# Moving operands at multiples of 1 KiB in SBUF, weight tiles 64 bytes past one, small tiles in a pool of their own

## The chip, the cores and the metric

The kernel runs on one core of one Trainium2 chip. The metric is the device time of one execution in microseconds (us). Before the change it is 2237.5 us, the median of three runs that lie between 2237.05 and 2237.68 us.

## The reference

The reference is a decoder trunk of two layers for one sequence of 256 tokens and width 2048. Layer 0 mixes with a short convolution and a gated linear attention, layer 1 with a dilated sliding-window attention of 16 heads; each is followed by an MLP of width 8192 with a squared ReLU, and a last RMSNorm ends it. What costs time is the weight matrices: about 400 MB of float32 weights, each used once, against 256 token columns.

```python
def reference(x, norm_mix_g, norm_mlp_g, final_norm_g, hyb_w_in, ..., mlp_w1, mlp_w2):
    for layer in range(DEPTH):
        h = rmsnorm(x, norm_mix_g[layer])
        if layer % 2 == 0:
            mix = conv_gla_mixer(h, hyb_w_in[e], ..., hyb_w_out[e])
        else:
            mix = dilated_attention(h, attn_w_qkv[o], attn_w_o[o])
        x = x + mix
        x = x + squared_relu_mlp(rmsnorm(x, norm_mlp_g[layer]), mlp_w1[layer], mlp_w2[layer])
    return rmsnorm(x, final_norm_g)
```

## The kernel before

Activations stand transposed in SBUF: 128 features of a k-block on the partitions, the 256 tokens along them. A float32 product is built from three products in the type float32r. Each value is split into a high part, rounded to float32r, and a low part, the rest; the kernel adds high by high, high by low and low by high in PSUM. So each activation block is a tile of 512 columns, 256 high and 256 low (2 KiB in a partition): `xs0` to `xs15` for the input of a mixer or of an MLP's first product, `ys0` to `ys15` for a mixer's output, and `hs0` to `hs15`, in the same places as `ys`, for a chunk of the MLP's hidden layer.

The weights come in steps of 128 x 1024 float32 (512 KiB, 4 KiB in a partition). For each of 770 steps SP issues the load into a ring of four `raw` tiles (line 114), ScalarE copies it rounded into a `wh` tile (line 119), VectorE subtracts that from the raw values into a `wl` tile (line 125); `wh` and `wl` are rings of five, filled four steps ahead of TensorE. Their order is that of the Python loop over `steps` at the end of `trunk_kernel`; a manual schedule keeps every engine in the order in which the program was written.

TensorE's work is nearly all in three forms, which all issue through the helper at line 128:

- `sub_a` (tile `acc` in the profile): a 128 x 128 piece of `wh` or `wl` is the stationary operand and the 256 high or low columns of an activation tile are the moving one. A step has eight such pieces and each takes three matmuls, in the order (`wh`, high), (`wh`, low), (`wl`, high): 24 matmuls a step.
- `sub_b` (tile `accv`), for the value projections: the roles are exchanged. 128 token columns of `xs` are stationary, 512 columns of `wh` or `wl` (2 KiB) move.
- `sub_g` (tile `accg`), as `sub_a`, for the gate projection and the last quarter of the last product.

```python
    def three(p, wh, wl, rhs, start, stop):
        hi, lo = rhs[:, :T], rhs[:, T:]
        mm(p, wh, hi, start, False)
        mm(p, wh, lo, False, False)
        mm(p, wl, hi, False, stop)
```

An MLP goes in four chunks: four groups of eight steps make 2048 hidden features from `xs` (768 matmuls), then four groups of eight steps take these, as `hs`, into the output (768 matmuls). The output projections of the two mixers read `ys` (768 matmuls each). All other products read `xs`.

Where a tile lies in a partition is set by the pools, one after the other in the order in which they are opened, and inside a pool by the order in which tiles are first asked for; each tile's length is rounded up to 32 bytes. The pool `const` holds `vec`, `cm` and `ones` (424, 1024 and 4 bytes), then `x`, `xs`, `ssq`, the two buffers of `rc` (8 bytes each, line 246), `rb`, `rb2` and `ys`; the pool `wts` with the rings follows, then `tmp`.

Of the kernel before, what the change touches and what calls it, by code (L numbers as in the profile page):

```python
# [11 lines left out]
F32 = mybir.dt.float32  # L12
# [6 lines left out]
P = 128  # L19
# [17 lines left out]
N_VEC = 106  # L37
# [12 lines left out]
def trunk_kernel(ctx: ExitStack, tc, xin, vecs, w_in, w_gate, w_gate2, w_out, w_qkv, w_o, w1, w2, w2f,  # L50
# [2 lines left out]
    pe, dve, act, pool = nc.tensor, nc.vector, nc.scalar, nc.gpsimd  # L53
    PSUM = bass.MemoryType.PSUM

    const = ctx.enter_context(tc.tile_pool(name="const", bufs=1))
    wts = ctx.enter_context(tc.tile_pool(name="wts", bufs=1))
    tmp = ctx.enter_context(tc.tile_pool(name="tmp", bufs=2))
# [5 lines left out]
    def bank(name):  # L64
        return psum.tile([P, 512], F32, tag="ps", name=name)


    vec = const.tile([P, N_VEC], F32, name="vec")
    cm = const.tile([P, 2, P], F32, name="cm")
    ident, cums = cm[:, 0, :], cm[:, 1, :]  # L70
    ones = const.tile([P, 1], F32, name="ones")
    x = const.tile([P, NK, T], F32, name="x")

    gpool = tc.alloc_tile_pool(name="gla", bufs=1)
# [52 lines left out]
    def mm(out_, lhsT, rhs, start, stop):  # L127
        pe.matmul(out_, lhsT=lhsT, rhs=rhs, start=start, stop=stop, skip_group_check=True)  # L128
# [95 lines left out]
    R = {}  # L224

    def rsqrt_cols(dst, src, scale, n):

        v = tmp.tile([P, 8], F32, tag="rv", name="rv")[:, :n]
        a = tmp.tile([P, 8], F32, tag="ra", name="ra")[:, :n]
        dve.tensor_scalar(v, src, scale, EPS, op0=OP.mult, op1=OP.add)  # L230
        act.activation(a, v, AF.Sqrt)
        dve.reciprocal(dst, a)
        dve.tensor_tensor(a, dst, dst, op=OP.mult)
        dve.tensor_tensor(a, a, v, op=OP.mult)
        dve.tensor_scalar(a, a, -0.5, 1.5, op0=OP.mult, op1=OP.add)
        dve.tensor_tensor(dst, dst, a, op=OP.mult)

    def norm_factor(last=False):

        p = bank("pss")  # L240
        for tt in range(2):
            for a in ssq["all"]:
                mm(p[:, tt:tt + 1], a[:, tt * P:(tt + 1) * P], ones, a is ssq["all"][0],
                   a is ssq["all"][-1])
        yield 1
        c = R["c"] = const.tile([P, 2], F32, tag="rc", bufs=2, name="rc")
        rsqrt_cols(c, p[:, :2], 1.0 / D, 2)
        yield 7
        p = bank("prb")
        for tt in range(2):  # L250
            pe.matmul(p[:, tt * P:(tt + 1) * P], lhsT=c[:, tt:tt + 1].to_broadcast([P, P]),
                      rhs=ident, start=True, stop=True)
        R["ps"] = p
        if last:
            return
        yield 1
        b = R["b"] = const.tile([P, T], F32, tag="rb", bufs=2, name="rb")
        act.activation(b, p[:, :T], AF.Copy)
        b2 = R["b2"] = const.tile([P, T], F32, tag="rb2", bufs=2, name="rb2")
        dve.tensor_tensor(b2, b, b, op=OP.mult)  # L260
        yield 1
# [17 lines left out]
    def residual(k, p, col=None, last=False, mlp=False):  # L279
        if mlp:  # L280
            t = tmp.tile([P, T], F32, tag="t", bufs=3, name="t")
            dve.tensor_tensor(t, p, R["b2"], op=OP.mult)  # L282
            p = t
        dve.tensor_tensor(x[:, k, :], x[:, k, :], p, op=OP.add)  # L284
        if col is not None:
            def rest():
                if last:
                    if k == 0:
                        fp = ctx.enter_context(
                            tc.tile_pool(name="fin", bufs=1, reuse_waits="tile"))  # L290
                        xf["x"] = fp.tile([P, NK, T], F32, name="xf")
                    if k == NK - 1:
                        sq = tmp.tile([P, T], F32, tag="sq", name="sq")
                        act.activation(sq, x[:, k, :], AF.Square)
                        ssq["all"].append(sq)
                    else:
                        square_sum(k)
                    act.activation(xf["x"][:, k, :], x[:, k, :], AF.Copy,
                                   scale=vec[:, col + k:col + k + 1])
                else:  # L300
                    scale_split(k, col)
                    square_sum(k)
                if k == NK - 1 and not last:
                    spawn(norm_factor(), 15)
            later.append(rest)
# [395 lines left out]
    def first_norm():  # L701
        for k in range(12, NK):
            square_sum(k, 12)
            yield 2
        ssq["all"] = [ssq["a"], ssq["p"]]
        yield 8
        yield from norm_factor()
# [43 lines left out]
    for _ in norm_factor(last=True):  # L751
        pass
# [97 lines left out]
```

## Time and profile before

| what | value |
|---|---|
| median of three runs | 2237.5 us |
| the profiled execution's own time | 2238.15 us |
| its span in the profile | 2236.2 us |
| TensorE matmuls busy | 2220.1 us, 99% of the span, 18390 records |
| TensorE weight loads busy | 2188.7 us, 98% |
| VectorE busy | 1326.2 us, 59% |
| ScalarE busy | 1039.4 us, 46% |
| DMA | 411.86 MB, mean 184 GB/s |

The span reaches from the first to the last instruction of the program; the time of an execution has some 2 us around it. A matmul's busy time is modelled to its end and overlaps with that of the next ones, so the pace of TensorE is read from the starts of the matmuls and from their counts, and not from the mean length of one. Where the listing of the timeline merges neighbours, a row's start is that of the first of them.

### The profile page before, as it was taken

The numbers are of one execution on the slowest core, as the hardware profiler recorded it, in microseconds if no ns is written. First come the engines' busy times: TensorE is split into PE (matmuls) and PEld (weight loads), VectorE is DVE, ScalarE is ACT, GpSimd is POOL, SyncE is SP. The second block draws the span as 40 slices with busy tenths as digits, with TensorE's granted clock in tenths as the row PEclk, the third lists the DMA queues.
The fourth block names the chain that finished last, engine by engine and source line by source line (L and its number), as shares of the span: only waits on it lengthen the run. The fifth ranks groups of instructions, "written<-read, shape, count | busy, mean of one in ns | idle before, by whom it ended". The sixth has DMA issues, their size and how long they took to land.

```text
span 2236.2 us, 43375 instructions
## 1 busy us (share of the span) xinstructions
PE 2220.1 (99%) x18390; PEld 2188.7 (98%) x18390; DVE 1326.2 (59%) x1809; ACT 1039.4 (46%) x1414; POOL 67.2 (3%) x70
## 2 busy tenths in 40 slices
PE   9999999999999999999999999999999999999997
PEld 8999999999999999999999999999999999999997
DVE  7666666555555555556665655565555555555555
ACT  6555545453444354345444444455434434534453
POOL 4001120000000000000000000000000000000000
PEclk9999999999999999999999999999999999999999
DMA  7555565566565656665655555556566666566653
GB/s 259 160 170 168 169 192 178 191 190 194 173 207 186 186 182 199 181 196 175 195 187 171 174 181 164 179 179 197 182 189 187 198 180 190 188 190 187 196 182 114
DMA packets 114405, 411.86 MB, mean 184 GB/s; under 512 B 12817, under 2 KB 13201, under 8 KB 114210
## 3 DMA queue, kind: packets, MB, share of 16 engines
q1 hardware_dynamic: 113760, 408.47, 58.1%
q8 instruction: 144, 2.36, 0.4%
q10 hardware_dynamic: 450, 0.61, 0.1%
q14 instruction: 51, 0.42, 0.1%
HBM read 406.94 MB, written 2.10 MB: 183 GB/s over the span
## 4 chain that ended last, share of the span: by engine, by line
PE 98%; DVE 1%; DMA 1%; issue 0%; SPq 0%; ACT 0%; DVEq 0%; ACTq 0%
PE acc L128 88%; PE accv L128 6%; PE accg L128 1%; PE psc L445 1%; PE pao L128 0%; DVE wl L125 0%; DVE xs L199 0%; DMA raw<-w_in 0%; PE pqk L580 0%; PE po L128 0%; PE ppt L598 0%; DVE xf L756 0%; DMA x<-xin 0%; PE pqk L579 0%; PE pos L128 0%
## 5 line engine op out<-in xcount | busy, mean ns | idle before, releaser
L125 DVE TENSOR_TENSOR wl<-raw,wh 128x1024 fp32r<-128x1024 f32 (+1 forms) x771 | 939.6, 1229 | 756.0 <-ACT wh L119 754.8
L119 ACT ACTIVATE wh<-raw 128x1024 fp32r<-128x1024 f32 (+1 forms) x771 | 810.6, 1056 | 903.9 <-PE acc L128 801.5
L128 PE MATMUL acc<-xs,wh 128*128 128x256 f32 x6400 | 1101.2, 277 | 0.1
L128 PEld LDWEIGHTS acc<-xs,wh 128*128 128x128 f32 x6400 | 965.8, 188 | 1.8 <-ACT wh L119 0.8
L128 PE MATMUL acc<-xs,wl 128*128 128x256 f32 x3200 | 885.2, 277 | 2.8 <-DVE wl L125 2.8
L128 PE MATMUL acc<-hs,wh 128*128 128x256 f32 x3968 | 714.4, 283 | 0.0
L128 PEld LDWEIGHTS acc<-hs,wh 128*128 128x128 f32 x3968 | 618.8, 192 | 0.0
L128 PEld LDWEIGHTS acc<-xs,wl 128*128 128x128 f32 x3200 | 601.0, 188 | 4.4 <-DVE wl L125 4.4
L128 PE MATMUL acc<-hs,wl 128*128 128x256 f32 x1984 | 561.5, 283 | 0.0
L128 PEld LDWEIGHTS acc<-hs,wl 128*128 128x128 f32 x1984 | 380.8, 192 | 0.0
L128 PE MATMUL acc<-ys,wh 128*128 128x256 f32 x1024 | 185.3, 284 | 0.0
L128 PEld LDWEIGHTS acc<-ys,wh 128*128 128x128 f32 x1024 | 159.8, 192 | 0.1
L128 PE MATMUL acc<-ys,wl 128*128 128x256 f32 x512 | 144.9, 283 | 0.0
L128 PE MATMUL accv<-wh,xs 128*128 128x512 f32 x384 | 122.0, 399 | 0.0
L271 DVE TENSOR_TENSOR hs<-u,hs 128x256 fp32r<-128x256 f32 x128 | 54.4, 425 | 79.0 <-ACT hs L270 79.0
L128 PEld LDWEIGHTS acc<-ys,wl 128*128 128x128 f32 x512 | 98.2, 192 | 0.0
L270 ACT ACTIVATE hs<-u 128x256 fp32r<-128x256 f32 x128 | 53.3, 417 | 71.0 <-DVE u L622 71.0
L128 PEld LDWEIGHTS accv<-wh,xs 128*128 128x128 f32 x384 | 70.3, 188 | 14.5 <-issue 0.8
L128 PE MATMUL accv<-wl,xs 128*128 128x512 f32 x192 | 75.5, 393 | 0.0
L284 DVE TENSOR_TENSOR x<-x,t 128x256 f32<-128x256 f32 x128 | 54.4, 425 | 4.4
L622 DVE TENSOR_TENSOR u<-u 128x256 f32<-128x256 f32 x128 | 53.5, 418 | 0.0
L282 DVE TENSOR_TENSOR t<-acc,rb 128x256 f32<-128x256 f32 x124 | 51.7, 417 | 0.0
(148 smaller groups left out, 793.8 us busy)
## 6 DMA issues: line engine op xcount, KB each, us to landing
raw<-w SPq DMA_DIRECT2D x504, 512.0 KB, 4.2
raw<-w_qkv SPq DMA_DIRECT2D x96, 512.0 KB, 3.6
raw<-w_in SPq DMA_DIRECT2D x95, 512.0 KB, 3.8
raw<-w_out SPq DMA_DIRECT2D x32, 512.0 KB, 3.8
raw<-w_o SPq DMA_DIRECT2D x32, 512.0 KB, 3.6
raw<-w2f SPq DMA_DIRECT2D x8, 512.0 KB, 3.8
x<-xin SPq DMA_DIRECT2D x8, 256.0 KB, 5.9
out_dram<-xf SPq DMA_DIRECT2D x7, 256.0 KB, 2.3
```

What stands on the lines that cost most here:

```text
L119: act.activation(his[s][:, c], raws[s][:, c], AF.Copy)
L125: dve.tensor_tensor(los[s][:, c], r[:, c], his[s][:, c].bitcast(F32), op=OP.subtract)
L128: pe.matmul(out_, lhsT=lhsT, rhs=rhs, start=start, stop=stop, skip_group_check=True)
L270: act.activation(t[:, :T], v, AF.Copy)
L271: dve.tensor_tensor(t[:, T:], v, t[:, :T].bitcast(F32), op=OP.subtract)
L282: dve.tensor_tensor(t, p, R["b2"], op=OP.mult)
L284: dve.tensor_tensor(x[:, k, :], x[:, k, :], p, op=OP.add)
L445: pe.matmul(p[:, (2 * h + tt) * P:(2 * h + tt + 1) * P], lhsT=l[:, h, c], rhs=r[:, h, c], start=True, stop=True)
L622: dve.tensor_tensor(u, u, u, op=OP.mult)
```

## The change

No instruction is added, removed or moved on any engine, and no wait is changed; only addresses in SBUF differ. A pool `small` is opened first and takes `vec`, `cm`, `ones` and the `rc` buffers. A tile of 88 float32 that nothing reads fills it up to a multiple of 1 KiB, and another of 16 float32 (64 bytes) stands at the head of the pool of the weight rings.

```diff
@@ -53,6 +53,9 @@
+    small = ctx.enter_context(tc.tile_pool(name="small", bufs=1))
     const = ctx.enter_context(tc.tile_pool(name="const", bufs=1))
     wts = ctx.enter_context(tc.tile_pool(name="wts", bufs=1))
     tmp = ctx.enter_context(tc.tile_pool(name="tmp", bufs=2))
@@ -65,10 +68,12 @@
-    vec = const.tile([P, N_VEC], F32, name="vec")
-    cm = const.tile([P, 2, P], F32, name="cm")
+    vec = small.tile([P, N_VEC], F32, name="vec")
+    cm = small.tile([P, 2, P], F32, name="cm")
     ident, cums = cm[:, 0, :], cm[:, 1, :]
-    ones = const.tile([P, 1], F32, name="ones")
+    ones = small.tile([P, 1], F32, name="ones")
+    small.tile([P, 88], F32, name="fill")
+    wts.tile([P, 16], F32, name="fill2")
     x = const.tile([P, NK, T], F32, name="x")
@@ -243,7 +248,7 @@
-        c = R["c"] = const.tile([P, 2], F32, tag="rc", bufs=2, name="rc")
+        c = R["c"] = small.tile([P, 2], F32, tag="rc", bufs=2, name="rc")
```

Where tiles begin, in bytes past a multiple of 1 KiB. All tiles named in a row have lengths that are multiples of 1 KiB, so each buffer of a row begins at the same remainder; a piece of a weight tile begins there or 512 bytes further, and so do the two 128-column pieces of a high or low part that `sub_b` loads.

| tiles | before | after |
|---|---|---|
| `x`, `xs` and `ssq` | 608 | 0 |
| `rb`, `rb2`, `ys` and `hs` | 672 | 0 |
| `raw`, `wh` and `wl` | 672 | 64 |
| `sq` and `u` in `tmp` | 736 | 128 |
| `v` of the value projections | 864 | 256 |
| `osq` and most other GLA tiles | 864 or 896 | 256 or 288 |

Before, `rc` takes two times 32 bytes between `ssq` and `rb`, which is why `ys` begins 64 bytes later in its KiB than `xs`.

## Rows read from the trace of the kernel before

**Rows 1.** The page's busy times: engine, us, share of the span, instructions.
```profile
PE 2220.1 (99%) x18390; PEld 2188.7 (98%) x18390; DVE 1326.2 (59%) x1809; ACT 1039.4 (46%) x1414; POOL 67.2 (3%) x70
```
**Rows 2.** The page's chain that ended last: shares by engine, then by line.
```profile
PE 98%; DVE 1%; DMA 1%; issue 0%; SPq 0%; ACT 0%; DVEq 0%; ACTq 0%
PE acc L128 88%; PE accv L128 6%; PE accg L128 1%; PE psc L445 1%; PE pao L128 0%; DVE wl L125 0%; DVE xs L199 0%; DMA raw<-w_in 0%; PE pqk L580 0%; PE po L128 0%; PE ppt L598 0%; DVE xf L756 0%; DMA x<-xin 0%; PE pqk L579 0%; PE pos L128 0%
```
**Rows 3.** Groups of TensorE's matmuls: busy us, mean ns, idle before.
```profile
L128 PE MATMUL acc<-xs,wh 128*128 128x256 f32 x6400 | 1101.2, 277 | 0.1
L128 PE MATMUL acc<-xs,wl 128*128 128x256 f32 x3200 | 885.2, 277 | 2.8 <-DVE wl L125 2.8
L128 PE MATMUL acc<-hs,wh 128*128 128x256 f32 x3968 | 714.4, 283 | 0.0
L128 PE MATMUL acc<-hs,wl 128*128 128x256 f32 x1984 | 561.5, 283 | 0.0
L128 PE MATMUL acc<-ys,wh 128*128 128x256 f32 x1024 | 185.3, 284 | 0.0
L128 PE MATMUL acc<-ys,wl 128*128 128x256 f32 x512 | 144.9, 283 | 0.0
L128 PE MATMUL accv<-wh,xs 128*128 128x512 f32 x384 | 122.0, 399 | 0.0
L128 PE MATMUL accv<-wl,xs 128*128 128x512 f32 x192 | 75.5, 393 | 0.0
L128 PE MATMUL accg<-hs,wh 128*128 128x256 f32 x128 | 23.1, 283 | 0.0
...
L128 PE MATMUL accg<-hs,wl 128*128 128x256 f32 x64 | 18.1, 283 | 0.0
```
**Rows 4.** Timeline of TensorE where an MLP chunk's halves meet: start, length, instruction.
```profile
584.87 0.40 PE L128 MATMUL acc<-xs,wh 128*128 128x256 f32 x2
...
671.92 0.39 PE L128 MATMUL acc<-hs,wh 128*128 128x256 f32 x2
...
764.07 0.40 PE L128 MATMUL acc<-xs,wh 128*128 128x256 f32 x2
```
**Rows 5.** Timeline of TensorE in a value projection.
```profile
1124.30 0.39 PE L128 MATMUL accv<-wl,xs 128*128 128x512 f32 x1
1124.53 0.62 PE L128 MATMUL accv<-wh,xs 128*128 128x512 f32 x2
...
1127.73 0.39 PE L128 MATMUL accv<-wl,xs 128*128 128x512 f32 x1
```
**Rows 6.** Stretches inside the chunk's halves, and the ends: busy us, PEclk, DMA share, GB/s.
```profile
590.00:670.00 80.00, 80.00 (x709) 80.00 (x707) 43.87 (x54) 38.80 (x54) 0.00 (x0) 1.00 0.62 197
680.00:760.00 80.00, 80.00 (x669) 80.00 (x669) 42.99 (x53) 29.64 (x28) 0.00 (x0) 1.00 0.63 192
...
0.00:40.00 40.00, 35.36 (x254) 32.02 (x255) 31.65 (x40) 25.68 (x42) 22.75 (x28) 1.00 0.78 263
...
2222.00:2236.20 14.20, 2.70 (x17) 2.23 (x15) 6.76 (x17) 1.02 (x3) 0.00 (x0) 0.62 0.41 148
```
**Rows 7.** Timeline of weight loads: eight in a row whose matmuls have one column.
```profile
138.85 0.97 PEld L128 LDWEIGHTS pos<-ones,osq 128*128 128x128 f32 x8
139.74 0.19 PEld L128 LDWEIGHTS acc<-xs,wh 128*128 128x128 f32 x1
```
**Rows 8.** Who waited for whom: us in total, times, longest.
```profile
ACT wh L119 <- PE acc L128: 801.5, 479, 2.1
DVE wl L125 <- ACT wh L119: 754.8, 551, 3.2
```

## The prediction

> **What bounds the kernel now.** I read the busy times first, then the chain that ended last, then TensorE's groups, then the timeline at the places where one kind of matmul follows another. TensorE is busy for 99% of the span with matmuls and for 98% with weight loads [rows 1], and the chain lies on it for 98%, 88% on `acc` and 6% on `accv` [rows 2]. The reader is to see that there is almost no wait to remove: before the costliest groups of `acc` it idled 0.1 and 2.8 us in all [rows 3]. ScalarE waited 801.5 us for TensorE and VectorE 754.8 us for ScalarE [rows 8], so the weights are ready ahead of need. So the time is the number of matmuls by the pace at which they start, and addresses alone can change only that pace.
>
> The pace is read from starts. An MLP's half chunk of 768 matmuls on `xs` starts at 584.87 and the next half, on `hs`, at 671.92: 87.05 us, 113.35 ns each. The 768 on `hs` end at 764.07: 92.15 us, 120.0 ns each [rows 4]. The counts of two stretches of 80 us say the same, 709 against 669 [rows 6], and so do the mean lengths, 277 ns on `xs` and 283 or 284 on `hs` and `ys` [rows 3]. The instruction is the same, and so are the rings of weights, VectorE's busy time (43.87 and 42.99 us) and the clock: the granted clock is 1.00 in both [rows 6], which is its level of 2.4 GHz, at which 256 columns need 106.7 ns. What differs is the address: `xs` begins 608 bytes past a KiB and the weights 672, while `hs` and `ys` begin at 672 like the weights. The excess over the columns is 6.7 ns for `xs` and 13.3 for `hs`: one unit and two units of 6.7 ns, that is 16 columns or 64 bytes.
>
> In a value projection fifteen matmuls of 512 columns lie between 1124.30 and 1127.73, 228.7 ns each [rows 5], against 213.3 for their columns: an excess of 15.3 ns, although a weight load has twice the time there. So a part of the excess grows with the length of the moving operand. That fits a moving operand which straddles a border of its memory: 1 KiB from 608 or 672 crosses one KiB border, 2 KiB from 672 cross two. The second unit on `hs` then is the load of the next weights that begins at the same place in its KiB as the stream.
>
> **The change part by part.** No instruction, wait or buffer count differs, so there is nothing to price but the pace, by group.
>
> The range for the new pace: below, the columns alone, 106.7 ns. Above, as far as weight loads bound it, the nearest row is eight loads in a row under matmuls of one column, which start from 138.85 to 139.74: 111 ns each [rows 7]. I take the middle, 109 ns, since neither end is shown for this form. The Trainium skill, TensorE: Matmul & The Clock Gate, section "Wait — 56ns, not 53.3ns?", states columns by 2.4 GHz plus about 2.5 ns for a warm matmul; its figure would be an estimate of 109.2 ns here, and no row of this kernel has that pace for this form.
>
> - `hs`, `ys` and the gate-shaped last product: 3968 + 1984 + 1024 + 512 + 128 + 64 = 7680 matmuls [rows 3]. They lose both units: 120.0 to 109 ns is 11.0 by 7680, 84.5 us. Bounds 9.0 (69 us) and 13.3 (102 us).
> - `xs`: 6400 + 3200 = 9600 matmuls [rows 3], with the 48 of the gate projection 9648; the first 240 lie in the first 40 us, where TensorE waits for its first tiles (35.36 us busy for 254 matmuls [rows 6]), and gain nothing. 9408 by 113.35 - 109 = 4.35 ns is 40.9 us. Bounds 2.35 (22 us) and 6.68 (63 us).
> - `accv`: 384 + 192 = 576 matmuls [rows 3]. Their moving operands are now 2 KiB from 64, which still cross two borders, and they begin 64 bytes after `xs` as before. I take nothing; bounds 0 and the whole excess, 8.8 us.
> - Other tiles (`x`, `v`, GLA and attention tiles) move too, but the chain has 1% or less on their lines [rows 2]. Nothing; the 14.2 us behind the last product, with 2.70 us of matmuls [rows 6], stay.
> - Cover: a step of 24 matmuls shrinks from 2.72 or 2.88 us to 2.62. VectorE is busy 43.87 of 80 us on `xs`, ScalarE 38.80, the DMA engines 62% at 197 GB/s [rows 6]; 4% faster than now on `xs` that is 57%, 50% and 65%, so none becomes the bound. Were it otherwise, VectorE's `wl` would be late first: it already released TensorE in the 2.8 us of waits [rows 3].
>
> The sum is 84.5 + 40.9 = 125.4 us. From the profiled execution's 2238.15 us that leaves 2112.8; the median stands 0.65 us below that execution, so **2112 us**. With all lower bounds of the gain (69 + 22) it is 2146, with all upper ones (102 + 63 + 9) 2063.
>
> **The rivals.**
>
> *Only the distance between the two starts counts.* `xs` shows one unit at 64 bytes behind the weights, `hs` two at 0. After the change everything stands 64 behind, so `hs` and `ys` come down to 113.35 ns and `xs` stays: 7680 by 6.65 is 51 us, **2186 us**. For it speaks that 113.35 is the only faster pace that a row shows, and that this distance is kept exactly. Against it, that `accv`, at another distance and with the weight load in half of its time, has more excess and not less.
>
> *Slower: stream and load still meet, and now on `xs` too.* The unit of the clash may be a cell of 128 bytes and not one of 64. In such cells 608 and 672 lie apart (512 to 639, 640 to 767) and 672 with 672 in one, as the two paces want it; but 0 and 64 lie in one cell, 0 to 127. Then all `acc` run at two units, 120.0 ns: 9408 by 6.65 is 63 us more on `xs` and no gain on `hs`, **2300 us**. The point from which it decides is the cell's size: 64 or less, no loss; 128 or more with a border between 608 and 672, this loss. For it: the two paces bear it out. Against: it needs exactly 128, since in cells of 256 or 512 bytes 608 and 672 would share one too.
>
> *Addresses do nothing.* The difference between the halves could come from something that goes with the stage. The time is then 2237.5 us. Against it: `ys`, in the output projections of the mixers, has the pace of `hs` although other work runs beside it [rows 3]. The Trainium skill has a rule that speaks against this change: SBUF — State Buffer, sections "SBUF: two separate sides" and "Who interferes with whom", gives TensorE two independent read ports, one for the moving operand and one for weight loads, says that a load takes nothing from the running matmul, and that TensorE never waits on anyone. By that rule the sum would be nothing; the two paces of one form [rows 4] do not agree with it as it stands.
>
> **How the numbers follow.** Forecast (both units go, 2063 to 2146): 0.45, since the excess of `accv` asks for a part that goes with the moving operand's length. Distance only (2186): 0.34. A gain on a part of the groups, anywhere between: 0.04. Nothing: 0.08. Slower: 0.09. About 0.2% is what a measurement of this kernel can tell from no change, 4.5 us. So faster 0.83, same 0.08, slower 0.09. The range reaches from 2062, with all bounds of the gain, to 2195, a little past the distance case; it leaves out the cases without gain and the slower one, 0.17, and some of the edges. The forecast's own range is 2063 to 2146.
>
> **What would show it.** Starts in an MLP's half chunk: 768 matmuls in about 84 us on `xs` and on `hs` alike (81.9 to 85.3) is the forecast; 87.05 on both is the distance case; 92.15 on both the slower one; 87 and 92 as before, nothing. `accv` should stay near 229 ns; if it falls by a unit, it is the start's place in a 64-byte line and not the KiB border that costs. If one of the halves shows idle time before `wl` instead, the cover was too thin. The prediction is wrong if `xs` keeps its 113.35 ns.

## The result

The changed kernel takes 2186.1 us, the median of four runs (2185.71 to 2186.57), against 2237.59 us of the kernel before, run beside it: a ratio of 0.977, 95% interval 0.9753 to 0.9787, or 51.5 us less. The forecast of 2112 us asked for 125 us, nearly two and a half times as much. The measured time is that of the first rival, in which only the distance between the two starts counts (2186 us).

The page's busy times of the changed kernel, then its groups of TensorE's matmuls (busy us, mean ns of one, idle before):

```profile
PE 2168.6 (99%) x18390; PEld 2137.3 (98%) x18390; DVE 1323.4 (61%) x1809; ACT 1038.8 (48%) x1414; POOL 66.9 (3%) x70
```
```profile
L133 PE MATMUL acc<-xs,wh 128*128 128x256 f32 x6400 | 1100.8, 277 | 0.1
L133 PE MATMUL acc<-xs,wl 128*128 128x256 f32 x3200 | 885.1, 277 | 2.2 <-DVE wl L130 2.2
L133 PE MATMUL acc<-hs,wh 128*128 128x256 f32 x3968 | 675.0, 276 | 0.0
L133 PE MATMUL acc<-hs,wl 128*128 128x256 f32 x1984 | 547.6, 276 | 0.0
L133 PE MATMUL acc<-ys,wh 128*128 128x256 f32 x1024 | 175.3, 277 | 0.0
```

Beside [rows 3], `xs` stands where it stood (277 ns; 1100.8 against 1101.2 us), and `hs` and `ys` came down from 283 and 284 to 276 and 277. Idle time did not grow: 2.2 us before the `wl` group. The timeline of TensorE at the same two borders of an MLP chunk as in [rows 4]:

```profile
573.76 0.28 PE L133 MATMUL acc<-xs,wh 128*128 128x256 f32 x1
...
660.80 0.28 PE L133 MATMUL acc<-hs,wh 128*128 128x256 f32 x1
...
747.84 0.28 PE L133 MATMUL acc<-xs,wh 128*128 128x256 f32 x1
```

Both halves now take 87.04 us, 113.3 ns a matmul. On `xs` that is the old pace (87.05 us), on `hs` 5.11 us less than the 92.15 of before. Ten such groups of 768 matmuls (7680 in all, with `ys` and the last product) make 51.1 of the 52.0 us by which the span fell, from 2236.2 to 2184.2. The value projections did not move, fifteen matmuls in 3.43 us or 228.7 ns each, as in [rows 5]:

```profile
1097.83 0.39 PE L133 MATMUL accv<-wl,xs 128*128 128x512 f32 x1
...
1101.26 0.39 PE L133 MATMUL accv<-wl,xs 128*128 128x512 f32 x1
```

Stretches of 75 us inside the two halves (busy us with instructions of PE, PEld, DVE, ACT and POOL, granted clock, DMA share, GB/s) have the same number of matmuls now, where [rows 6] had 709 and 669 in 80 us. The cover held: VectorE is busy for 57% and 59% of them, against 55% and 54%.

```profile
580.00:655.00 75.00, 75.00 (x664) 75.00 (x663) 42.54 (x52) 36.31 (x52) 0.00 (x0) 1.00 0.64 197
665.00:740.00 75.00, 75.00 (x664) 75.00 (x663) 44.37 (x55) 30.20 (x30) 0.00 (x0) 1.00 0.64 197
```

ScalarE still waits for TensorE most of all, 62 us less than in [rows 8]:

```profile
ACT wh L124 <- PE acc L133: 739.5, 468, 2.1
DVE wl L130 <- ACT wh L124: 707.3, 521, 3.2
```

### The profile page after: what moved, and what is told of

Same layout as the page of the kernel before. It is cut to its first block, busy times and chain, and to the rows that moved or that the text cites. A ratio compares the mean times of both kernels' runs of the same rounds, so it can differ in the third digit from the quotient of the medians.

```text
span 2184.2 us, 43375 instructions
## 1 busy us (share of the span) xinstructions
PE 2168.6 (99%) x18390; PEld 2137.3 (98%) x18390; DVE 1323.4 (61%) x1809; ACT 1038.8 (48%) x1414; POOL 66.9 (3%) x70
## 4 chain that ended last, share of the span: by engine, by line
PE 98%; DVE 1%; DMA 1%; issue 0%; ACT 0%; SPq 0%; DVEq 0%; ACTq 0%
PE acc L133 88%; PE accv L133 6%; PE accg L133 1%; PE psc L450 1%; DMA raw<-w_in 1%; PE pao L133 0%; DVE wl L130 0%; PE pqk L585 0%; PE po L133 0%; PE ppt L603 0%; DVE xs L204 0%; DVE xf L761 0%; PE pqk L584 0%; PE pos L133 0%; PE pss L133 0%
## 5 line engine op out<-in xcount | busy, mean ns | idle before, releaser
L133 PE MATMUL acc<-xs,wh 128*128 128x256 f32 x6400 | 1100.8, 277 | 0.1
L133 PE MATMUL acc<-hs,wh 128*128 128x256 f32 x3968 | 675.0, 276 | 0.0
L133 PEld LDWEIGHTS acc<-hs,wh 128*128 128x128 f32 x3968 | 597.2, 188 | 0.0
L133 PE MATMUL acc<-hs,wl 128*128 128x256 f32 x1984 | 547.6, 276 | 0.0
L133 PEld LDWEIGHTS acc<-hs,wl 128*128 128x128 f32 x1984 | 372.4, 188 | 0.0
L133 PE MATMUL acc<-ys,wh 128*128 128x256 f32 x1024 | 175.3, 277 | 0.0
L133 PEld LDWEIGHTS acc<-ys,wh 128*128 128x128 f32 x1024 | 154.4, 188 | 0.1
```

## The experiments

In all of them "distance" is the start of a weight tile less the start of the moving tile. It is given modulo 512, since a weight piece begins 0 or 512 bytes past its tile's start (the third layout has 960 on `xs`, which stands as 448). A half is a group of 768 matmuls, timed from its first start to the first start of the next group.

### Other distances, four layouts

The same program with other lengths of the filling tiles, and a third one ahead of `rb`, so that `ys` and `hs` have one distance and `xs` another. For the first of the four:

```diff
-    wts.tile([P, 16], F32, name="fill2")
+    wts.tile([P, 8], F32, name="fill2")
...
+        if "b" not in R:
+            const.tile([P, 24], F32, name="fill3")
         b = R["b"] = const.tile([P, T], F32, tag="rb", bufs=2, name="rb")
```

> The weight tiles begin 32 bytes past the remainder of ys and hs, and 128 bytes past that of xs; nothing else differs from the changed kernel. Theory A (the second unit is paid only where stream and load begin at the same remainder): both halves of an MLP chunk at 113.35 ns, 87.05 us for 768 matmuls, total 2186 us. Theory B (paid within one 64-byte line): hs and ys at 120 ns, 92.15 us, xs at 113.35, total 2237 us. Theory C (the first unit goes too once the distance is large enough): xs at 109 ns or less, 83.7 us a half, total 2146 us or less where hs follows A.

> Weights 96 bytes past ys and hs, 256 past xs. A: both halves at 113.35 ns, total 2186 us. B: the same, since both distances are over a line. C: one or both halves under 111 ns; xs at 109 would take 41 us off, hs at 109 33 us.

> Weights 32 bytes ahead of ys and hs and 64 ahead of xs, if remainders repeat after 512 bytes as the equal paces of the 512-byte pieces suggest. A: both halves at 113.35 ns, 2186 us. B: hs and ys at 120 ns, xs at 113.35, 2237 us. C: under 111 ns in one half.

> Weights 192 bytes past ys and hs, 384 past xs. A and B: both halves at 113.35 ns, 2186 us. C: under 111 ns in one half or both.

They took 2283.25, 2276.91, 2245.10 and 2271.62 us, one run each beside 2237.53 us of the kernel before: all slower than it, and none as any of the three theories had it. Timeline of the second layout (96 and 256) at the borders of a chunk: 92.15 us on `xs`, 120.0 ns, and 90.11 on `hs`, 117.3 ns.

```profile
595.09 0.28 PE L133 MATMUL acc<-xs,wh 128*128 128x256 f32 x1
...
687.24 0.28 PE L133 MATMUL acc<-hs,wh 128*128 128x256 f32 x1
...
777.35 0.28 PE L133 MATMUL acc<-xs,wh 128*128 128x256 f32 x1
```

In the third (480 and 448) one and the same form of half takes 90.45 us in one chunk and 87.04 in the next, on `xs`, and 92.16 and then 89.6 on `hs`:

```profile
589.80 0.28 PE L133 MATMUL acc<-xs,wh 128*128 128x256 f32 x1
...
680.25 0.28 PE L133 MATMUL acc<-hs,wh 128*128 128x256 f32 x1
...
772.41 0.28 PE L133 MATMUL acc<-xs,wh 128*128 128x256 f32 x1
...
859.45 0.28 PE L133 MATMUL acc<-hs,wh 128*128 128x256 f32 x1
...
949.06 0.28 PE L133 MATMUL acc<-xs,wh 128*128 128x256 f32 x1
```

Within a half the pace does not drift. Two stretches of the slower half on `xs` (busy us with matmuls of PE, granted clock, DMA share, GB/s) count 342 matmuls each; two of the faster one, 775 to 815 and 815 to 855, count 355 each:

```profile
600.00:640.00 40.00, 40.00 (x342) 1.00 0.57 180
640.00:680.00 40.00, 40.00 (x342) 1.00 0.60 197
```

So theory A (only equal starts clash) and B (only starts within a line) fall: of these eight distances, none of them 0 or 64, none holds the 113.3 ns throughout. C (some distance frees the first unit too) found nothing under 113.3 ns.

### More distances, and whether they repeat

The same edit with other lengths.

> Weights 320 bytes past ys and hs, 416 past xs (so far: 0 and 128 and 256 give 120 ns, 32, 96, 192 and 384 give 117 to 119, 64 gives 113.35). If the pattern repeats after 256 bytes, 320 is as 64: hs at 113.35 ns, 87.05 us a half, and 416 is as 160, near 118. If only 64 on either side of the start is good, both lie at 117 to 120 ns, total 2270 to 2285 us.

> Weights 160 bytes past ys and hs, 288 past xs. If distances repeat after 256 bytes, 160 is as 416 was (119.6 to 120.8 ns) and 288 as 32 (118.3). If not, 288 may take any value from 113.35 to 120.

> Weights 224 bytes past ys and hs, 352 past xs. If distances repeat after 256 bytes, 224 is as 480 was (116.7 ns in most halves, 120.0 in others) and 352 as 96 (117.3). If not, either may reach 113.35.

They took 2249.09, 2284.64 and 2262.56 us. Timeline of the first of them: `hs` at distance 320 is at 87.06 us, the pace of 64, and `xs` at 416 at 92.15.

```profile
589.77 0.28 PE L133 MATMUL acc<-xs,wh 128*128 128x256 f32 x1
...
681.92 0.28 PE L133 MATMUL acc<-hs,wh 128*128 128x256 f32 x1
...
768.98 0.28 PE L133 MATMUL acc<-xs,wh 128*128 128x256 f32 x1
```

All distances together, with the pace of a matmul in ns from the halves of the MLP chunks (in brackets the run; two values where halves differ):

| distance | pace | distance + 256 | pace |
|---|---|---|---|
| 0 | 120.0 (before, `hs`) | 256 | 120.0 (second layout) |
| 32 | 118.3 (first) | 288 | 118.3 |
| 64 | 113.3 (before, `xs`; after, both) | 320 | 113.3 |
| 96 | 117.3 (second) | 352 | 117.3 to 120.0 |
| 128 | 120.0 (first) | 384 | 118.7 (fourth) |
| 160 | 120.0 | 416 | 120.0 |
| 192 | 117.8 (fourth) | 448 | 113.3 and 117.8 (third) |
| 224 | 116.7 | 480 | 116.7 and 120.0 (third) |

The pace repeats with 256 bytes, exactly at 0, 32, 64 and 160, and within the values that one layout itself shows at 96, 192 and 224. At 128 the halves differ by 1.3 ns, but outside of them each layout has the other's value too: the first runs at 118.7 ns in the input projection of layer 0, the fourth at 120.0 in the first product of layer 1's MLP. Only 64 holds the lowest pace throughout.

The values are few. They are 113.3 ns and 113.3 plus a half, three fifths, two thirds, three quarters, four fifths or the whole of one unit of 6.7 ns, and a half keeps its value from its first matmuls to its last. Where a distance has more than one of them, something beside the distance picks one; these runs do not show what.

### The parts of the change alone

On the kernel before, the move of `rc` alone:

```diff
+    small = ctx.enter_context(tc.tile_pool(name="small", bufs=1))
     const = ctx.enter_context(tc.tile_pool(name="const", bufs=1))
...
-        c = R["c"] = const.tile([P, 2], F32, tag="rc", bufs=2, name="rc")
+        c = R["c"] = small.tile([P, 2], F32, tag="rc", bufs=2, name="rc")
```

> Of the change only the move of rc into a pool of its own, on the kernel before: xs, ys and the weights all begin at 672. If the distance of the starts decides: xs falls from 113.35 to 120.0 ns like hs, 92.15 us for every half, total 2300 us. If the place in the KiB decides and not the distance: hs stays at 120.0 and xs, which moves from 608 to 672, may go either way; if the KiB's borders decide, xs keeps its 113.35 and the total stays at 2237 us.

2296.80 us: `xs` fell to the pace of `hs` as the distance had it, 92.16 us for either half.

```profile
598.89 0.28 PE L129 MATMUL acc<-xs,wh 128*128 128x256 f32 x1
...
691.05 0.28 PE L129 MATMUL acc<-hs,wh 128*128 128x256 f32 x1
...
783.21 0.28 PE L129 MATMUL acc<-xs,wh 128*128 128x256 f32 x1
```

And with the 64 bytes in addition, still without the filling up to 1 KiB:

```diff
+    wts.tile([P, 16], F32, name="fill2")
     x = const.tile([P, NK, T], F32, name="x")
```

> Of the change only the move of rc and the 64 bytes ahead of the weights: all moving tiles at 672, all weights at 736, nothing at a multiple of 1 KiB, every matmul on a mixer's or an MLP's tile straddles a border. Distance decides: 113.35 ns on both, 2186 us, the same as the changed kernel. Multiples of 1 KiB are needed: slower than 2186 us by up to 51 us.

2186.66 us, median of four runs, a ratio to the kernel before of 0.9773 (95% interval 0.9757 to 0.979). That is the changed kernel's ratio, although every moving tile begins at 672 and straddles a border of 1 KiB. The halves take 87.04 us each:

```profile
573.68 0.28 PE L130 MATMUL acc<-xs,wh 128*128 128x256 f32 x1
...
660.72 0.28 PE L130 MATMUL acc<-hs,wh 128*128 128x256 f32 x1
...
747.76 0.28 PE L130 MATMUL acc<-xs,wh 128*128 128x256 f32 x1
```

So the move of `rc` and the 64 bytes are the whole effect. Multiples of 1 KiB do nothing for it.

### Shorter streams and shorter loads

The question was what holds the pace at 113.3 ns when the distance is right. These kernels leave parts of the sums out and serve only to read paces. In the changed layout, for all but the first k-block:

```diff
+            if n and g.src is w2:
+                a, q = g.rhs(n), p[:, :192]
+                mm(q, wh[:, c], a[:, :192], False, False)
+                mm(q, wh[:, c], a[:, T:T + 192], False, False)
+                mm(q, wl[:, c], a[:, :192], False, n == 15)
+                continue
+            if n and g.src is w1:
+                c = slice(kk * 512 + j * P, kk * 512 + j * P + 96)
+                three(p[:96, :], wh[:, c], wl[:, c], g.rhs(n), False, n == 15)
+                continue
```

> The changed layout; in the MLP products, for all but the first k-block of an accumulation, the matmuls on hs move 192 of the 256 columns and those on xs load 96 of the 128 weight columns, so parts of the sums are left out. What sets the last 113.35 ns? If the weight load does: hs stays near 111 to 113 ns, xs falls (to the columns' 106.7 ns or little more). If the stream of columns does: hs falls to about 87 ns (80 ns of columns and one unit), xs stays at 113.35. If both end together and meet in memory: both fall only in part.

> The changed layout; in the MLP products, for all but the first k-block, hs moves 192 columns under loads of 96 weight columns, and xs moves 256 under loads of 64; the rest of the sums is left out. If a load's time goes with its columns: hs falls from 112.0 ns (192 under 128) to 84 to 90. If a load takes its 112 ns whatever its columns: hs stays at 112. On xs, 113.35 with 64 columns as with 96 and 128 would mean that the stream sets it or that loads do not shorten; only together with a fall on hs does it mean the stream.

Timeline of the first of them, with 192 columns under full loads on `hs` and loads of 96 on `xs`, at the borders of a chunk:

```profile
574.12 0.30 PE L133 MATMUL acc<-xs,wh 128*128 128x256 f32 x1
...
661.22 0.28 PE L133 MATMUL acc<-hs,wh 128*128 128x256 f32 x1
...
747.23 0.30 PE L133 MATMUL acc<-xs,wh 128*128 128x256 f32 x1
```

The half on `xs` takes 87.10 us, the half on `hs` 86.01. In each, 48 matmuls are whole (the first k-block of each of its four groups). Where the short ones on `hs` follow one another, 156 of them lie between these two starts, 111.5 ns each:

```profile
685.13 0.36 PE L133 MATMUL acc<-hs,wh 128*128 128x192 f32 x2
...
702.53 0.39 PE L133 MATMUL acc<-hs,wh 128*128 128x192 f32 x2
```

Then, with 192 columns under loads of 96 on `hs`, and loads of 64 on `xs`:

```profile
556.83 0.30 PE L133 MATMUL acc<-xs,wh 128*128 128x256 f32 x1
...
643.90 0.28 PE L133 MATMUL acc<-hs,wh 128*128 128x256 f32 x1
...
713.68 0.30 PE L133 MATMUL acc<-xs,wh 128*128 128x256 f32 x1
```

`hs` falls to 69.78 us, and `xs` keeps 87.07. The short ones on `hs` take 88.7 ns each, 168 of them between these starts:

```profile
663.62 0.34 PE L133 MATMUL acc<-hs,wh 128*96 128x192 f32 x2
...
678.52 0.34 PE L133 MATMUL acc<-hs,wh 128*96 128x192 f32 x2
```

So two limits lie close together at distance 64. A full load of 128 weight columns takes 111.5 ns of TensorE's time and is shorter with fewer columns. The stream of 256 columns takes 113.3 whether the load beside it has 128, 96 or 64 columns. The runs took 2180.66 and 2055.56 us.

The same cut as in the first of these two, with all tiles at multiples of 1 KiB, so at distance 0 (the 64 bytes left out):

```diff
-    wts.tile([P, 16], F32, name="fill2")
```

> All moving tiles and all weights at multiples of 1 KiB, so distance 0 everywhere; in the MLP products hs moves 192 columns under full loads, xs 256 under loads of 96 columns (the rest left out). The output projections are whole: distance decides, ys at 120.0 ns; multiples of 1 KiB help by themselves, ys under 120. On hs: if the clash delays the stream only, the shorter stream hides it and hs is at 112, the load's time as at distance 64; if it delays the load, hs is at 115 to 120. On xs: 120 if a shorter load meets the stream just as often, less if the clash goes with the columns loaded.

```profile
589.93 0.30 PE L133 MATMUL acc<-xs,wh 128*128 128x256 f32 x1
...
679.16 0.28 PE L133 MATMUL acc<-hs,wh 128*128 128x256 f32 x1
...
765.22 0.30 PE L133 MATMUL acc<-xs,wh 128*128 128x256 f32 x1
```

2226.49 us. The output projection, which is whole, takes 92.16 us for its 768 matmuls, 120.0 ns: the distance decides, and multiples of 1 KiB do not help by themselves.

```profile
321.62 0.28 PE L133 MATMUL acc<-ys,wh 128*128 128x256 f32 x1
...
413.78 0.28 PE L133 MATMUL acc<-xs,wh 128*128 128x256 f32 x1
```

On `hs` (86.06 us; the short ones, where they follow one another, start 111.5 ns apart) the clash is gone from sight, since the load's 111.5 ns cover the shorter stream. On `xs` (89.23 us) 96 columns a load leave 116.0 ns of the 120.0. So the clash delays the stream and not the load, and a shorter load clashes less.

### What the last 6.7 ns are

The changed layout with loads of 64 weight columns and three widths of the moving operand, 224 on `xs`, 128 on `hs`, 512 in the value projections:

```diff
+            m = 128 if g.src is w2 else 224
+            if n and (g.src is w2 or g.src is w1):
+                c = slice(kk * 512 + j * P, kk * 512 + j * P + 64)
+                a, q = g.rhs(n), p[:64, :m]
...
+        if n:
+            hi, lo, p = hi[:, :64], lo[:, :64], p[:64, :]
```

> The changed layout; for all but the first k-block, loads of 64 weight columns, so that the loads are short, and moving operands of 224 columns on xs, 128 on hs and 512 in the value projections (the rest left out). If the last unit is a rate of the float32r stream, 17/16 of the columns at 2.4 GHz: 99.2 ns on xs, 56.7 on hs unless 64-column loads (about 56) and starts add to it, 226.7 in the value projections. If it is one unit of 6.7 ns for each matmul: 100.0, 60.0 and 220.0. If it is a border of 1 KiB: 93.3 ns on xs and 53.3 on hs, which no longer reach one, and 226.7 in the value projections, which cross two.

Timeline in a stretch of each kind, 39 matmuls on `xs`, 9 on `hs` and 12 in a value projection:

```profile
562.15 0.36 PE L133 MATMUL acc<-xs,wh 128*64 128x224 f32 x2
...
566.14 0.36 PE L133 MATMUL acc<-xs,wh 128*64 128x224 f32 x2
...
641.51 0.23 PE L133 MATMUL acc<-hs,wl 128*64 128x128 f32 x1
...
642.05 0.22 PE L133 MATMUL acc<-hs,wl 128*64 128x128 f32 x1
...
971.53 0.39 PE L133 MATMUL accv<-wl,xs 128*64 128x512 f32 x1
...
974.27 0.39 PE L133 MATMUL accv<-wl,xs 128*64 128x512 f32 x1
```

That is 102.3, 60.0 and 228.3 ns a matmul, an excess over the columns of 9.0, 6.7 and 15.0 ns; with 256 columns it was 6.7 and with 192 (under loads of 96) it was 8.7. The border of 1 KiB is out: 128 columns from the start of a KiB reach none and still pay 6.7 ns. A fixed unit fits 128 and 256 columns and misses 512 by 8 ns; the rate of 17/16 fits 512 to 2 ns and misses 128 by 3.

The runs before this one show what the 2 ns are. In a value projection 128 columns of `xs` are loaded and 512 of `wh` or `wl` move, and its pace follows the distance too: 228.7 ns where the load's start lies 64 bytes below the stream's (before and after), 233.3 where it lies 288 below (weights 288 past `xs`). With the move of `rc` alone both begin at 672, and eighteen matmuls take 4.08 us, 226.7 ns each. No layout went below that, and only those with distance 0 or 256 on `xs` came within 0.5 ns of it:

```profile
1153.69 0.39 PE L129 MATMUL accv<-wl,xs 128*128 128x512 f32 x1
...
1157.77 0.39 PE L129 MATMUL accv<-wl,xs 128*128 128x512 f32 x1
```

So equal starts, among the worst for 256 moving columns, are the best for 512, and what then stays is 13.3 ns: 1/16 of the columns' time, as the 6.7 ns of 256 columns are. The rate of 17/16 fits both and misses 128, 192 and 224 columns by 3 to 4 ns. The own pace of those three was read at distance 64 alone; whether another distance brings them nearer to it was not tried. Why the stream takes 17/16 is open, and no layout that was tried took it away. In the run with three widths (1935.60 us) `hs` then waits for `wl`, so its halves are no measure.

## Why the prediction was wrong

- **What bounds the kernel** was right: the pace alone changed, no idle time came or went, and the cover held.
- **The size of the two units** was right, and so was the reading of the second: it belongs to the distance between the load and the stream (though it comes at other distances than equal starts too). The term of 7680 matmuls was mis-sized. It was 11.0 ns each for both units, 84.5 us; measured were the 6.7 ns of one unit, 51.1 us.
- **The step that failed** is the one in which the excess of `accv` "fits a moving operand which straddles a border of its memory". From it came the 40.9 us on `xs`, which measured nothing, and the other 33 us on `hs`. The excess does grow with the moving length (15.3 ns at 512 columns, of which 13.3 stay at equal starts), but it goes with no border: `xs` moved from 608 to 0 and kept 113.3 ns, and the layout with everything at 672 and 736 has the same time as the change.
- **The bound from above was drawn from the wrong row.** The 111 ns of back-to-back loads [rows 7] bound the loads, and the runs confirm that (111.5 ns under short streams). But the nearest row for the stream was the 113.35 ns of `xs` itself, the same form at the distance that the change keeps, and the range of 106.7 to 111 left it out.
- **The rivals.** Distance only was the case that came: 2186 us forecast and 2186.1 measured. What was held against it, the larger excess of `accv`, is no clash for the most part: 2 of its 15.3 ns go with the distance. Cells of 128 bytes are excluded, since 0 with 64 runs at 113.3. That addresses do nothing is excluded: with the move of `rc` alone `xs` went from 113.3 to 120.0 ns, with no instruction changed.
- **What no rival said:** distance 64 (or 320) is a narrow good spot for this form. The kernel before had `xs` on it by the accident of two 32-byte buffers, and seven other pairs of distances made it slower than before, by 8 to 47 us.

The Trainium skill, SBUF — State Buffer, section "Who interferes with whom", gives TensorE two independent read ports, one for the moving operand and one for weight loads, and has it waiting on no one. The runs differ: a load holds up the stream beside it, by 6.7 ns a matmul between distances 64 and 0. The Trainium skill, TensorE: Matmul & The Clock Gate, section "LDWEIGHTS (loading the stationary operand)", gives a load the time of its columns by 1.2 GHz, an estimate of 106.7 ns for 128, and says that columns count. The fall from 111.5 to 88.7 ns with 96 columns agrees in kind (the 88.7 may be the stream's); the full load showed 111.5.

## What to carry to other kernels

Where matmuls run back to back with a weight load for each, read the pace from starts for each tile that moves, and set the paces beside the tiles' addresses: a difference of a few ns between two groups of one form is worth 2% here. What counts is the start of the weights less the start of the moving tile, with a period of 256 bytes in what was tried. 64 was best for 256 float32r columns, and equal starts or 128 or 160 the worst; for 512 columns equal starts were best, so the good distance has to be measured for each form. A small buffer put between two big ones shifts everything behind it, so keep small tiles in a pool of their own, and measure the distance again after any change of the pools.

## What was not expected of the hardware

- The pace at one layout is not always one value: at distance 448 halves of the same form took 90.45 us in one chunk and 87.04 in the next, and the same values came again in the second layer.
- The clash is not worst at equal starts alone: 128 and 160 bytes also cost the full 120.0 ns, and 32 bytes 118.3. With 512 moving columns equal starts have the least, 226.7 ns.
- A full weight load holds TensorE for 111.5 ns even when the stream beside it needs less, so at 113.3 ns the stream and the load are within 1.8 ns of each other: by an estimate from these two, any better layout for this form would have at most 17088 by 1.8 ns, about 31 us, to win.
